# Six hand-overs to the FFN's down projection, a sixth weight buffer, and a first rstd by columns in a two-layer trunk

## The chip, the cores and the metric

The kernel runs on one core of a Trainium2 chip. The metric is the device time of one execution in microseconds; less is better. A core has a matrix engine (TensorE, PE in the profile; PEld is its weight load, which overlaps), a vector engine (VectorE, DVE), an engine for activation functions (ScalarE, ACT), a general engine (GpSimd, POOL) and a sync engine (SP) that here only issues loads and stores. Each engine takes its own instructions in the order of the program, and waits on semaphores for the results of the others. Matmuls write to PSUM, eight banks of 128 x 512 f32 values; everything else lives in SBUF.

## What is computed

The input is 512 tokens of 1024 channels. Two layers each have a mixer and a gated FFN with a short causal convolution, each behind an RMS norm and added to the residual; a final RMS norm closes. Cut to what matters here:

```python
def rms_norm(x, g):
    y = x * lax.rsqrt(jnp.mean(x * x, axis=-1, keepdims=True) + EPS)
    return y * g

def gated_conv_ffn(x, w_gate, w_up, conv_w, conv_b, w_down):   # w_gate, w_up: 1024 x 2816
    g = jnp.einsum('bsd,df->bsf', x, w_gate)
    g = causal_dwconv3(g, conv_w) + conv_b
    up = jnp.einsum('bsd,df->bsf', x, w_up)
    return jnp.einsum('bsf,fd->bsd', jax.nn.silu(g) * up, w_down)

for layer in range(2):
    xn = rms_norm(h, norm_mix[layer])
    h = h + (mixer_a_and_b(xn) if layer == 0 else mixer_c(xn))   # each with an output projection
    hn = rms_norm(h, norm_ffn[layer])
    h = h + gated_conv_ffn(hn, w_ffn_gate[layer], w_ffn_up[layer], conv_ffn[layer],
                           b_conv_ffn[layer], w_ffn_down[layer])
return rms_norm(h, final_norm)
```

Mixer A and B of layer 0 begin with one input projection; its last 512 columns, z, are normalized, pooled over windows of 2, 4, 8 and 16 tokens and multiplied by small matrices.

## The kernel before, in words

The residual stands transposed in SBUF: `h[k]`, eight tiles of 128 channels x 512 tokens. Every f32 operand of a matmul is split into a high and a low part (`hi`, `lo`: ScalarE rounds, VectorE subtracts, or a DMA adds), and a product is three matmuls: hi x hi, hi x lo, lo x hi (`mm3`, lines 134 to 137). A norm is not applied first: `Norm.add` splits h times the gain into `hg[k]`, and the factor rstd of a token is multiplied in after the projection. `Norm.square` sums the squares over the eight tiles into `ssq`, ScalarE squaring and GpSimd adding (L190, L191). With `apart=True` the last square stays in a tile of its own. From there, `rstd` makes all 512 factors in one row form, the same on all partitions, with two matmuls against a matrix of ones (L200, L201) and full-width VectorE passes (`inv_sqrt`, L242 to L251). `rstd_tokens` makes them as four columns, with small matmuls against a column of ones (L211, L212), and `rstd_spread` turns these into the row form by four transposes (L219) and a copy (L222). Layer 0's mixer uses `rstd`; both FFNs use the other two. `z_done` evacuates the z groups: it takes rstd at its first call, copies the bank (L406), multiplies (L407) and pools.

The FFN's 2816 hidden channels are 22 tiles, worked on in pairs f = 0, 2, ... 20. `Ffn.hidden(f)` makes one pair's activations:

- f = 0 (`direct`, not normed): 96 matmuls of gate and up weights with unnormalized `hg`, during which the columns of rstd are made and spread. Then `normalize` is issued for four pairs of channel tiles (it rewrites `hg` with the normalized input and prepares sums), and only then `rest()`, the evacuation: bank times rstd (L555), three taps of the convolution (L504, L506), silu (L512), times rstd on GpSimd (L558), times the up bank (L561), and the split into a_hi and a_lo (`act`, L261, L263).
- f = 2 (`direct`, normed): 96 matmuls, which need the normalized `hg`.
- f >= 4 (`seven`): the up product by seven half-size products (L663), the gate product as before.

`PARTS` says after which pairs the down projection runs: its entries (a, b) are ranges of tiles. In layer 0 `project` multiplies the part's activations with its down weights and adds into `h` (L306), in two halves of four output tiles. In layer 1 `group8` does the same with tokens as rows, eight outputs, and adds into `y` (L923). Both go through the first len - tail tiles with all outputs interleaved, then finish output by output; tail is 4.

What sets the order: the program's text is not the order of execution. A scheduler orders each engine's instructions ahead of time, and tile pools bound what it may do. A pool's tile with `bufs=n` is a ring, handed out in the order of the text: the next request waits until the use n requests before is over. So the matmul banks (`mm`, seven in the ring, and one more, `aux`) are handed out in the order of the text, and so are the split weights (`whi` and `wlo`, five each), the raw weights (four) and the activations (`ahi`, `alo`, six). On the engines nothing overtakes at run time. The queues: SP issues the loads of weights, GpSimd the DMAs that add for some low parts (L123, L595).

```python
PARTS = ((0, 6), (6, 12), (12, 18), (18, 22))
```

Of the kernel before, what the change touches and what calls it, by code (L numbers as in the profile page):

```python
# [8 lines left out]
F32 = mybir.dt.float32  # L9
F32R = mybir.dt.float32r  # L10
BF16 = mybir.dt.bfloat16
AF = mybir.ActivationFunctionType
ALU = mybir.AluOpType
PSUM = bass.MemoryType.PSUM

P = 128
D = 1024
S = 512
# [6 lines left out]
PAD = 16  # L25
# [5 lines left out]
def tile_trunk(ctx: ExitStack, tc: tile.TileContext, x, norm_mix, norm_ffn, final_norm,  # L31
# [16 lines left out]
    def aux_bank(name):  # L48
        return ps_aux.tile([P, 512], F32, tag="aux", name=name)
# [10 lines left out]
    small = cp.tile([P, LINE], F32, name="small")  # L60
    ones = small[:, :1]
    nc.gpsimd.memset(ones, 1.0)
    ones_r = cp.tile([P, P], F32R, name="ones_r")
    nc.gpsimd.tensor_copy(ones_r, ones.to_broadcast([P, P]))
    def params0():
        return params("0", [
            ("ca", conv_rows(conv_a[0]), 12), ("psc", rows_of(pool_scale[0]), 4),
# [17 lines left out]
    def params(layer, rows_, queue=nc.sync):  # L85
        rows = sum(n for _, _, n in rows_)
        pk = cp.tile([P, P], F32, tag="pk", bufs=1, name=f"pk{layer}")
        at, views = 0, {}
        for key, ap, n in rows_:
            queue.dma_start(pk[at : at + n, :], ap)  # L90
            views[key] = at
            at += n
        ps = aux_bank(f"prm_ps{layer}")
        nc.tensor.transpose(ps[:, :rows], pk[:rows, :], ident[:rows, :rows])
        sb = cp.tile([P, P], F32, tag=f"prm{layer}", name=f"prm{layer}")
        nc.vector.tensor_copy(sb[:, :rows], ps[:, :rows])

        def col(key, i):
            return sb[:, views[key] + i : views[key] + i + 1]

        return col
# [15 lines left out]

    def summed(raw, a, b, name):

        hi = wp.tile([P, a, b], F32R, tag="whi", bufs=5, name=f"whi_{name}")  # L120
        lo = wp.tile([P, a, b], F32R, tag="wlo", bufs=5, name=f"wlo_{name}")
        nc.scalar.activation(lo, raw, AF.Copy, scale=-1.0)  # L122
        nc.gpsimd.dma_start(lo, raw, accum_op=ALU.add)  # L123
        nc.scalar.activation(hi, raw, AF.Copy)
        return hi, lo

    def parts(raw, a, b, name):
        hi = wp.tile([P, a, b], F32R, tag="whi", bufs=5, name=f"whi_{name}")
        lo = wp.tile([P, a, b], F32R, tag="wlo", bufs=5, name=f"wlo_{name}")
        nc.scalar.activation(hi, raw, AF.Copy)  # L130
        nc.vector.tensor_tensor(lo, raw, hi.bitcast(F32), ALU.subtract)  # L131
        return hi, lo
# [6 lines left out]
    def group(name, outs, ks, lhs, rhs, tail, on_done, before=None, at_end=None):  # L139

        banks = {}
        head = len(ks) - tail
        order = [(i, j) for i in range(head) for j in outs]
        order += [(i, j) for j in outs for i in range(head, len(ks))]
        at = -1
        for i, j in order:
            if i > at and before is not None:
                before(ks[i])
            at = max(at, i)
            if j not in banks:  # L150
                banks[j] = mm_bank(f"{name}_{j}")
            mm3(banks[j], lhs(ks[i], j), rhs(ks[i], j), i == 0, i == len(ks) - 1)
            if i == len(ks) - 1 and at_end is None:
                on_done(j, banks[j])
        if at_end is not None:
            at_end()
            for j in outs:
                on_done(j, banks[j])
# [9 lines left out]
    class Norm:  # L168
# [13 lines left out]
        def square(self, k, order=lambda ins: ins):  # L182
            if self.n == 0:
                order(nc.scalar.activation(self.ssq, h[k], AF.Square))
            elif self.n == NK - 1 and self.apart:
                self.last = tp.tile([P, S], F32, tag="last", bufs=1, name=f"last_{self.name}")
                order(nc.scalar.activation(self.last, h[k], AF.Square))
            else:
                sq = tp.tile([P, S], F32, tag="sq", name=f"sq_{self.name}{k}")
                order(nc.scalar.activation(sq, h[k], AF.Square))  # L190
                nc.gpsimd.tensor_tensor(self.ssq, self.ssq, sq, ALU.add)  # L191
            self.n += 1

        def rstd(self):
            ps = aux_bank(f"ss_{self.name}")
            hi = tp.tile([P, S], F32R, tag="sq", name=f"ssh_{self.name}")
            lo = tp.tile([P, S], F32R, tag="sq", name=f"ssl_{self.name}")
            nc.scalar.activation(hi, self.ssq, AF.Copy)
            nc.vector.tensor_tensor(lo, self.ssq, hi.bitcast(F32), ALU.subtract)
            nc.tensor.matmul(ps, ones_r, hi, start=True, stop=False)  # L200
            nc.tensor.matmul(ps, ones_r, lo, start=False, stop=True)  # L201
            r = tp.tile([P, S], F32, tag="rstd", name=f"rstd_{self.name}")
            inv_sqrt(r, ps, S, self.name)
            return r

        def rstd_tokens(self):

# [139 lines left out]
    def mixer0():  # L347
        nonlocal prm0
        w = w_in_even[0]
        with tc.tile_pool(name="m0", bufs=1) as mp:  # L350
            prm_mix = params("mix", [("mix", rows_of(norm_mix[0]), NK)], nc.scalar)
            norm = Norm("m0", lambda k: prm_mix("mix", k))
            zchunks = {}
            xt = {}

# [12 lines left out]
            def turn(k):  # L368
                ps = mm_bank(f"xt_ps{k}")
                for t in range(NT):  # L370
                    nc.tensor.transpose(ps[:, t * P : (t + 1) * P], xt[k][:, t, :], ident)
                if k in raws:
                    raw, a, b, name = raws.pop(k)
                    hi = wp.tile([P, a, b], F32R, tag="whi", bufs=5, name=f"whi_{name}")
                    lo = wp.tile([P, a, b], F32R, tag="wlo", bufs=5, name=f"wlo_{name}")
                    for i in range(a):
                        zchunks[k + i] = hi[:, i, :], lo[:, i, :], raw[:, i, :]
                whi, wlo, wraw = zchunks[k]
                inorder(nc.scalar.activation(whi, wraw, AF.Copy))
                inorder(nc.vector.tensor_copy(h[k], ps))  # L380
                g = prm_mix("mix", k)
                inorder(nc.scalar.activation(hg[k][0], h[k], AF.Copy, scale=g))
                inorder(nc.vector.tensor_tensor(wlo, wraw, whi.bitcast(F32), ALU.subtract))
                inorder(nc.vector.scalar_tensor_tensor(
                    hg[k][1], h[k], g, hg[k][0].bitcast(F32), op0=ALU.mult, op1=ALU.subtract))
                norm.square(k, inorder)
                if k == 0:
                    load(6, 2)
# [8 lines left out]
            pooled = {}  # L397
            rstd = [None]

            def z_done(g, ps):  # L400
                if rstd[0] is None:
                    rstd[0] = norm.rstd()
                win = WINDOWS[g]
                z = mp.tile([P, S + LINE], F32, tag="z", bufs=2, name=f"z{g}")[:, :W]
                nc.gpsimd.memset(z[:, :PAD], 0.0)
                nc.scalar.copy(z[:, PAD:], ps)  # L406
                nc.vector.tensor_tensor(z[:, PAD:], z[:, PAD:], rstd[0], ALU.mult)  # L407
                s, step = z, 1
                while step < win:
                    s2 = mp.tile([P, S + LINE], F32, tag="zs", bufs=3, name=f"zs{g}_{step}")[:, :W]  # L410
                    lo_c = 2 * step - 1
                    nc.vector.tensor_tensor(s2[:, lo_c:], s[:, lo_c:], s[:, lo_c - step : W - step],
                                            ALU.add)
                    s, step = s2, 2 * step
                pl = mp.tile([P, S], F32, tag="pl", bufs=2, name=f"pl{g}")
                nc.vector.scalar_tensor_tensor(pl, s[:, PAD:], 1.0 / win, z[:, PAD:],
                                               op0=ALU.mult, op1=ALU.subtract)
                e = win - 1
                nc.vector.tensor_tensor(pl[:, :e], s[:, PAD : PAD + e], inv_pos[:, :e], ALU.mult)
                nc.vector.tensor_tensor(pl[:, :e], pl[:, :e], z[:, PAD : PAD + e], ALU.subtract)  # L420
                pooled[g] = split(mp, pl, f"pl{g}", tag="mix", bufs=8)
# [50 lines left out]
            return nxt  # L472


    PARTS = ((0, 6), (6, 12), (12, 18), (18, 22))
    HALF = S // 2
    NP = NK // 2
    PAIRS = [k for i in range(NP) for k in (i, i + NP)]
# [8 lines left out]
    class Ffn:  # L487
# [25 lines left out]
            return s  # L513

        def act(self, ft, s):
            self.acts[ft] = split(self.ap, s, f"a{self.layer}_{ft}", tag="a", bufs=6)

        def pair_weights(self, f, order, by_dma=""):

# [88 lines left out]
        def seven(self, f):  # L608
# [3 lines left out]
            stat = {}  # L612

            def pair(name):
                return [wp.tile([P, 2, 4, P], F32R, tag=f"w{x}", bufs=5, name=f"w{x}_{name}_{n}")
                        for x in ("hi", "lo")]

            def halves(hi, lo, src):
# [328 lines left out]

    def group8(name, ks, lhs, rhs, tail, on_done):
        banks = {}
        head = len(ks) - tail  # L950
        order = [(i, j) for i in range(head) for j in range(8)]
        order += [(i, j) for j in range(8) for i in range(head, len(ks))]
        for i, j in order:
# [40 lines left out]
```

## Time and profile before

| | us |
|---|---|
| median of 3 runs | 1012.66 (1012.38 to 1012.75) |
| the profiled execution | 1013.46 |
| its span, first to last instruction | 1011.5 |
| mean granted TensorE clock | 0.997 |

The profile is of one execution. A line of a group tells: line, engine, operation, output <- inputs, form, count | busy time, mean ns of one | the engine's idle time before, and what ended it. In order of time, a line tells start and duration, and in brackets the idle time before it and what ended it. One matmul of 128 x 512 lasts 0.39 us from start to end, but the next one starts 0.227 us after it: they are pipelined. Where the time goes on TensorE, largest groups:

| work | matmuls | busy us |
|---|---|---|
| gate products, `g`, L135 to L137 | 864 | 337 |
| down products, `d` and `dn`, L135 to L137 | 1056 | 411 |

The busy column counts each matmul's whole length, so overlapping ones of different groups count more than once.

| stretch, us | what runs |
|---|---|
| 0 to 147 | layer 0, mixer; 7.8 to 36 the z group, rstd ready at 44.7 |
| 147 to 491 | layer 0, FFN; first pair to 171.2, second to 193.0, pair f = 4 to 214, first down projection 214 to 246.8 |
| 491 to 645 | layer 1, mixer |
| 645 to 1004 | layer 1, FFN; second pair 673.0 to 694.9, first down projection 715.8 to 748.6 |
| 1004 to 1011.5 | final norm's end and the last store |

### The profile page before, as it was taken

To read this page: it belongs to the slowest core of one execution; us is meant where nothing else is said; L and a number is where in the kernel's file an instruction comes from. 1 tells how busy PE (TensorE), PEld (TensorE's weight loads), DVE (VectorE), ACT (ScalarE), POOL (GpSimd) and SP (SyncE) were. 2 spreads that over 40 slices of the span, in tenths; PEclk is the share of its full clock that TensorE was granted. 3 is DMA by queue.
4 is the path that set the end of the run, shared out by engine and by line. 5 is a ranking of instruction groups with operands and counts; after the bars stand their busy time and mean duration, and the time that the engine had idled before them with its cause. 6 is when DMAs were issued, how large, how long until landed. Compare 5 with 4: busy or idle time off the path is not lost.

```text
span 1011.5 us, 13009 instructions
## 1 busy us (share of the span) xinstructions
PE 998.6 (99%) x5169; PEld 853.3 (84%) x5169; DVE 612.6 (61%) x882; ACT 471.5 (47%) x685; POOL 90.0 (9%) x101
## 2 busy tenths in 40 slices
PE   9999999999999999999999999999999999999997
PEld 6788888888998899889878888888888988998885
DVE  5997458864557366636833645396745654763667
ACT  6423446642454266236645444575425623650553
POOL 3141021200000000000300001111000000000000
PEclk9999999999999999999999999999999999999998
DMA  7432235442444344434333123354424433442432
GB/s 239 151 104 84 84 99 143 113 146 71 125 117 143 87 119 132 126 84 125 131 120 104 63 90 98 96 121 117 146 63 126 135 116 89 141 127 82 122 87 83
DMA packets 79303, 114.98 MB, mean 114 GB/s; under 512 B 4004, under 2 KB 53388, under 8 KB 79244
## 3 DMA queue, kind: packets, MB, share of 16 engines
q1 hardware_dynamic: 73580, 98.96, 30.7%
q0 software_dynamic: 4320, 13.63, 7.3%
q10 hardware_dynamic: 1344, 1.58, 0.5%
q8 instruction: 40, 0.66, 0.3%
q14 instruction: 19, 0.16, 0.1%
HBM read 98.42 MB, written 2.10 MB: 99 GB/s over the span
## 4 chain that ended last, share of the span: by engine, by line
PE 95%; DVE 3%; ACT 1%; issue 1%; DMA 1%; POOL 0%; DVEq 0%; ACTq 0%; POOLq 0%
PE ua L663 10%; PE g L135 7%; PE g L136 6%; PE g L137 6%; PE ue L663 5%; PE d L136 4%; PE dn L137 4%; PE dn L135 4%; PE d L137 4%; PE d L135 4%; PE dn L136 4%; PE gu L135 3%; PE gu L137 3%; PE gu L136 3%; PE ub L663 3%; PE u L135 1%
## 5 line engine op out<-in xcount | busy, mean ns | idle before, releaser
L135 PE MATMUL g<-hgh,whi_g 128*128 128x512 f32 x288 | 112.5, 391 | 0.0
L136 PE MATMUL g<-hgl,whi_g 128*128 128x512 f32 x288 | 112.5, 391 | 0.0
L137 PE MATMUL g<-hgh,wlo_g 128*128 128x512 f32 x288 | 112.1, 389 | 0.0
L130 ACT ACTIVATE whi_g<-raw_g 128x1024 fp32r<-128x1024 f32 x40 | 42.1, 1053 | 93.6 <-PE dn L137 57.3
L136 PE MATMUL d<-a_lo,whi_d 128*128 128x512 f32 x176 | 68.6, 390 | 0.0
L135 PE MATMUL dn<-whi_dn,a_hi 128*128 128x512 f32 x176 | 68.6, 390 | 0.0
L136 PE MATMUL dn<-wlo_dn,a_hi 128*128 128x512 f32 x176 | 68.5, 389 | 0.0
L506 DVE SCALAR_TENSOR_TENSOR c<-rows,prm,c 128x512 f32<-128x512 f32 x88 | 68.1, 793 | 0.6
L137 PE MATMUL d<-a_hi,wlo_d 128*128 128x512 f32 x176 | 68.5, 389 | 0.0
L137 PE MATMUL dn<-whi_dn,a_lo 128*128 128x512 f32 x176 | 68.3, 389 | 0.0
L135 PE MATMUL d<-a_hi,whi_d 128*128 128x512 f32 x176 | 68.3, 390 | 0.0
L131 DVE TENSOR_TENSOR wlo_g<-raw_g,whi_g 128x1024 fp32r<-128x1024 f32 x40 | 48.8, 1221 | 28.3 <-ACT whi_g L130 28.3
L137 PEld LDWEIGHTS g<-hgh,wlo_g 128*128 128x128 f32 x288 | 54.1, 188 | 11.9 <-DVE wlo_g L131 0.5
L123 POOL DMA_DIRECT2D wlo_u<-raw_u x18 | 15.4, 857 | 536.3 <-ACT wlo_u L122 200.1
L135 PEld LDWEIGHTS g<-hgh,whi_g 128*128 128x128 f32 x288 | 54.2, 188 | 10.3
L136 PEld LDWEIGHTS g<-hgl,whi_g 128*128 128x128 f32 x288 | 54.2, 188 | 9.8
L620 DVE TENSOR_TENSOR wlo_a<-raw_u,whi_a 128x512 fp32r<-128x512 f32 x18 | 12.5, 692 | 82.6 <-ACT whi_a L619 82.6
L681 ACT COPY kept<-ua 128x256 f32<-128x256 f32 x54 | 19.8, 367 | 74.3 <-PE ua L663 74.3
L131 DVE TENSOR_TENSOR wlo_d<-raw_d,whi_d 128x1024 fp32r<-128x1024 f32 x22 | 26.9, 1221 | 35.1 <-ACT whi_d L130 35.1
L131 DVE TENSOR_TENSOR wlo_dn<-raw_dn,whi_dn 128x1024 fp32r<-128x1024 f32 x22 | 26.8, 1220 | 35.1 <-ACT whi_dn L130 35.1
L923 DVE TENSOR_TENSOR y<-dn,y 128x512 f32<-128x512 f32 x32 | 22.1, 689 | 42.9 <-PE dn L137 42.9
L619 ACT ACTIVATE whi_s<-s 128x1024 fp32r<-128x1024 f32 x36 | 38.1, 1057 | 19.9 <-PE d L136 14.2
(326 smaller groups left out, 2756.7 us busy)
## 6 DMA issues: line engine op xcount, KB each, us to landing
raw_u<-in_w_ffn_up_dram SPq DMA_DIRECT2D x36, 512.0 KB
raw_g<-in_w_ffn_gate_dram SPq DMA_DIRECT2D x36, 512.0 KB
raw_d<-in_w_ffn_down_dram SPq DMA_DIRECT2D x22, 512.0 KB
raw_dn<-in_w_ffn_down_dram SPq DMA_DIRECT2D x22, 512.0 KB
wlo_u<-raw_u POOLq DMA_DIRECT2D x18, 512.0 KB, 4.6
raw_oe<-in_w_out_even_dram SPq DMA_DIRECT2D x8, 512.0 KB
raw_g<-in_w_ffn_gate_dram SPq DMA_DIRECT2D x16, 256.0 KB
raw_u<-in_w_ffn_up_dram SPq DMA_DIRECT2D x16, 256.0 KB
```

Of the source, the lines that this page charges most:

```text
L123: nc.gpsimd.dma_start(lo, raw, accum_op=ALU.add)
L130: nc.scalar.activation(hi, raw, AF.Copy)
L131: nc.vector.tensor_tensor(lo, raw, hi.bitcast(F32), ALU.subtract)
L135: nc.tensor.matmul(ps, lhs[0], rhs[0], start=start, stop=False)
L136: nc.tensor.matmul(ps, lhs[0], rhs[1], start=False, stop=False)
L137: nc.tensor.matmul(ps, lhs[1], rhs[0], start=False, stop=stop)
L506: nc.vector.scalar_tensor_tensor(c, t[:, i : S + i], prm("cf", i * NF + ft), c, op0=ALU.mult, op1=ALU.add)
L619: nc.scalar.activation(hi, src, AF.Copy)
L620: nc.vector.tensor_tensor(lo, src, hi.bitcast(F32), ALU.subtract)
L663: nc.tensor.matmul(ps, l, r, start=at not in opened, stop=end, skip_group_check=True)
L681: nc.scalar.copy(kept[:, i, :], ps)
L923: nc.vector.tensor_tensor(dst, ps, dst, ALU.add)
```

## The change

`PARTS` has six entries. The first is the first pair alone, the others have four tiles. Since `len - tail` would be negative for the first, both loops take `max(0, ...)`. The activations' ring goes from six to four tiles, the rings of split weights from five to six. The matrix of ones and `rstd` are removed; layer 0's mixer takes `rstd_tokens` when the first z group is done and `rstd_spread` when the third is, and z's first two groups are only copied until then, and pooled after. The spare row of the last square and one of the parameter tiles share the space of others. Cut to its core:

```diff
-    ones_r = cp.tile([P, P], F32R, name="ones_r")
-    nc.gpsimd.tensor_copy(ones_r, ones.to_broadcast([P, P]))
...
-        sb = cp.tile([P, P], F32, tag=f"prm{layer}", name=f"prm{layer}")
+        sb = cp.tile([P, P], F32, tag="prm0" if layer == "0" else "prm1", name=f"prm{layer}")
...
     def parts(raw, a, b, name):
-        hi = wp.tile([P, a, b], F32R, tag="whi", bufs=5, name=f"whi_{name}")
-        lo = wp.tile([P, a, b], F32R, tag="wlo", bufs=5, name=f"wlo_{name}")
+        hi = wp.tile([P, a, b], F32R, tag="whi", bufs=6, name=f"whi_{name}")
+        lo = wp.tile([P, a, b], F32R, tag="wlo", bufs=6, name=f"wlo_{name}")
...
     def group(name, outs, ks, lhs, rhs, tail, on_done, before=None, at_end=None):
-        head = len(ks) - tail
+        head = max(0, len(ks) - tail)
...
             elif self.n == NK - 1 and self.apart:
-                self.last = tp.tile([P, S], F32, tag="last", bufs=1, name=f"last_{self.name}")
+                self.last = tp.tile([P, S], F32, tag="rstd", name=f"last_{self.name}")
...
-        def rstd(self):
-            ps = aux_bank(f"ss_{self.name}")
-            hi = tp.tile([P, S], F32R, tag="sq", name=f"ssh_{self.name}")
-            lo = tp.tile([P, S], F32R, tag="sq", name=f"ssl_{self.name}")
-            nc.scalar.activation(hi, self.ssq, AF.Copy)
-            nc.vector.tensor_tensor(lo, self.ssq, hi.bitcast(F32), ALU.subtract)
-            nc.tensor.matmul(ps, ones_r, hi, start=True, stop=False)
-            nc.tensor.matmul(ps, ones_r, lo, start=False, stop=True)
-            r = tp.tile([P, S], F32, tag="rstd", name=f"rstd_{self.name}")
-            inv_sqrt(r, ps, S, self.name)
-            return r
...
-            norm = Norm("m0", lambda k: prm_mix("mix", k))
+            norm = Norm("m0", lambda k: prm_mix("mix", k), apart=True)
...
+            zs = {}
+
+            def z_copy(g, ps):
+                zs[g] = mp.tile([P, S + LINE], F32, tag="z", bufs=2, name=f"z{g}")[:, :W]
+                nc.gpsimd.memset(zs[g][:, :PAD], 0.0)
+                nc.scalar.copy(zs[g][:, PAD:], ps)
+
             def z_done(g, ps):
-                if rstd[0] is None:
-                    rstd[0] = norm.rstd()
-                win = WINDOWS[g]
-                z = mp.tile([P, S + LINE], F32, tag="z", bufs=2, name=f"z{g}")[:, :W]
-                nc.gpsimd.memset(z[:, :PAD], 0.0)
-                nc.scalar.copy(z[:, PAD:], ps)
+                if g == 0:
+                    norm.rstd_tokens()
+                elif g == 2:
+                    rstd[0] = norm.rstd_spread()
+                    z_pool(0)
+                    z_pool(1)
+                z_copy(g, ps)
+                if g > 1:
+                    z_pool(g)
+
+            def z_pool(g):
+                win, z = WINDOWS[g], zs[g]
                 nc.vector.tensor_tensor(z[:, PAD:], z[:, PAD:], rstd[0], ALU.mult)
...
-    PARTS = ((0, 6), (6, 12), (12, 18), (18, 22))
+    PARTS = ((0, 2), (2, 6), (6, 10), (10, 14), (14, 18), (18, 22))
...
         def act(self, ft, s):
-            self.acts[ft] = split(self.ap, s, f"a{self.layer}_{ft}", tag="a", bufs=6)
+            self.acts[ft] = split(self.ap, s, f"a{self.layer}_{ft}", tag="a", bufs=4)
...
             def pair(name):
-                return [wp.tile([P, 2, 4, P], F32R, tag=f"w{x}", bufs=5, name=f"w{x}_{name}_{n}")
+                return [wp.tile([P, 2, 4, P], F32R, tag=f"w{x}", bufs=6, name=f"w{x}_{name}_{n}")
                         for x in ("hi", "lo")]
...
     def group8(name, ks, lhs, rhs, tail, on_done):
-        head = len(ks) - tail
+        head = max(0, len(ks) - tail)
```

The scheduler places the first part's down projection, in both layers, directly behind the first pair's 96 matmuls on TensorE and ahead of the second pair's.

More of the change, by code (lines that the diff above doesn't have):

```diff
@@ L127, in parts @@
     def parts(raw, a, b, name):
-        hi = wp.tile([P, a, b], F32R, tag="whi", bufs=5, name=f"whi_{name}")
-        lo = wp.tile([P, a, b], F32R, tag="wlo", bufs=5, name=f"wlo_{name}")
+        hi = wp.tile([P, a, b], F32R, tag="whi", bufs=6, name=f"whi_{name}")
+        lo = wp.tile([P, a, b], F32R, tag="wlo", bufs=6, name=f"wlo_{name}")
         nc.scalar.activation(hi, raw, AF.Copy)
@@ L373, in turn @@
                     raw, a, b, name = raws.pop(k)
-                    hi = wp.tile([P, a, b], F32R, tag="whi", bufs=5, name=f"whi_{name}")
-                    lo = wp.tile([P, a, b], F32R, tag="wlo", bufs=5, name=f"wlo_{name}")
+                    hi = wp.tile([P, a, b], F32R, tag="whi", bufs=6, name=f"whi_{name}")
+                    lo = wp.tile([P, a, b], F32R, tag="wlo", bufs=6, name=f"wlo_{name}")
                     for i in range(a):
```

## The prediction

> **What bounds the kernel now.** I read the page first, then TensorE's waits, then stretches of the two FFN stages, then single instructions in order of time where the change cuts in. First the page (busy us, share, instructions) and TensorE's waits (us in total, times, longest):
>
> ```profile
> span 1011.5 us, 13009 instructions
> ...
> PE 998.6 (99%) x5169; PEld 853.3 (84%) x5169; DVE 612.6 (61%) x882; ACT 471.5 (47%) x685; POOL 90.0 (9%) x101
> ```
>
> ```profile
> PE wst L764 <- POOL ws L757: 1.5, 1, 1.5
> ...
> PE z L135 <- ACT hgh L382: 1.0, 2, 0.8
> PE z L136 <- DVE hgl L384: 0.8, 1, 0.8
> ```
>
> TensorE is the bound: its last matmul starts at 1003.6, and it lacks work for about 5 us before that. No wait in either FFN is even listed. So nothing inside the FFNs can be gained by a faster hand-over or earlier weights, and any wait that the change puts on TensorE is paid in full, since no later idle time can pay it back. The stretches around the first two FFN pairs (us, then busy us of each engine; the clock is the column after POOL):
>
> ```profile
> 171.00:193.00 22.00, 22.00 (x99) 18.22 (x98) 22.00 (x34) 17.57 (x27) 6.98 (x6) 1.00 0.49 112
> 673.00:695.00 22.00, 22.00 (x99) 18.23 (x98) 22.00 (x34) 17.80 (x27) 6.96 (x6) 1.00 0.50 119
> 1004.00:1011.00 7.00, 0.00 (x0) 0.00 (x0) 3.24 (x10) 1.01 (x4) 0.00 (x0) 0.66 0.27 100
> ```
>
> In 171 to 193 TensorE runs the 96 matmuls of the second pair (f = 2), 21.8 us, or 0.227 us each. VectorE is just as full: it finishes the normalization and makes the first pair's activations. The second layer's 673 to 695 is the same to 0.02 us. In the last row the clock falls once TensorE is idle. Now the first pair's activations, start and duration in us:
>
> ```profile
> 170.99 0.39 PE L137 MATMUL gu<-hgh,wlo_u 128*128 128x512 f32 x1
> 171.21 0.39 PE L135 MATMUL gu<-hgh,whi_g 128*128 128x512 f32 x1
> ```
>
> ```profile
> 175.34 0.69 DVE L555 TENSOR_TENSOR rows<-gu,rstd_f 128x512 f32<-128x512 f32 x1
> ...
> 178.47 0.75 DVE L506 SCALAR_TENSOR_TENSOR c<-rows,prm,c 128x512 f32<-128x512 f32 x1
> ...
> 179.84 1.28 ACT L512 ACT_TABLE_LOAD   x1
> ...
> 181.13 0.72 ACT L512 ACTIVATE s<-c,prm 128x512 f32<-128x512 f32 x1
> ...
> 181.94 1.98 POOL L558 TENSOR_TENSOR s<-s,rstd_f 128x512 f32<-128x512 f32 x1 [1.50 <-ACT s L512]
> ```
>
> ```profile
> 185.10 0.63 ACT L261 ACTIVATE a_hi<-s 128x512 fp32r<-128x512 f32 x1 [1.05 <-DVE s L561]
> 185.76 0.73 ACT L512 ACTIVATE s<-c,prm 128x512 f32<-128x512 f32 x1
> 186.31 0.68 DVE L263 TENSOR_TENSOR a_lo<-s,a_hi 128x512 fp32r<-128x512 f32 x1
> ...
> 186.56 1.58 POOL L558 TENSOR_TENSOR s<-s,rstd_f 128x512 f32<-128x512 f32 x1 [2.65 <-ACT s L512]
> ...
> 189.35 0.62 ACT L261 ACTIVATE a_hi<-s 128x512 fp32r<-128x512 f32 x1
> ...
> 190.48 0.68 DVE L263 TENSOR_TENSOR a_lo<-s,a_hi 128x512 fp32r<-128x512 f32 x1
> ```
>
> At 171.21 the loads change from up weights to gate weights: the first pair's last matmul is out and the second pair begins. The first pair's two activations, each a high and a low part, are complete only at 191.2, 20 us later. Before the change nobody asks for them until 214, when the first down projection starts.
>
> **The change, part by part.** *The first part, (0, 2).* The down projection of part one needs only activations 0 and 1, and its 48 matmuls now stand on TensorE directly behind the first pair's 96 and ahead of the second pair's 96; so the built program orders them, in both layers. TensorE takes its instructions in order, so at 171.2 it waits for a chain that has just begun, and the 21.8 us of the second pair, its cover until now, is queued behind the wait.
>
> When is the chain done? VectorE has the same work ahead of L555 as before (the whole normalization of the pairs, with two weight splits), without a gap in the trace, so L555 stays at 175.3. The table load, silu, GpSimd product and first high part follow at the times shown: the other VectorE work put in between (two splits of down weights, 1.22 each, and L631, 0.69) is 3.1 us against 3.3 us now (L620, L131, L631, L633). So the first a_hi ends at 185.7. In the new order the taps of the second pair (L506, 1.78 at its longest) no longer stand between, so the second GpSimd product, ending 188.1, is taken up at once: product 0.68, high part 0.62, low part 0.68 bring the last low part to 190.1. Ten of the 48 matmuls fit in before that; the other 38 take 38 x 0.227 = 8.6 us, to 198.8. Unhindered, the 48 would be done at 171.2 + 10.9 = 182.1. So 16.7 us are lost.
>
> *The clock behind that wait.* TensorE does nothing for 14.5 us. At the end of the run the clock record falls to 0.5 within 2.3 us of the last matmul (hence 0.66 in the row above), and at the start the eight warming matmuls of 1.25 to 4.85 step by 0.43 us where they later would by half, full rate being recorded from 6.15, 4.9 us after the first. The fed matmuls resume at 185.8; full rate may come by 190.7. The few cold matmuls queued at 190 and the tail of the ramp cost 1.0 us as an estimate; bounds 0, and 2.5 if the ramp begins only at 190 and runs 4.9 us at half rate. [...]
>
> Bounds for one layer: below, the bare chain with no queue on VectorE or ScalarE (0.69 + 0.73 + 2 x 0.75 + 1.28 + 0.72 + 1.29 + 0.68 + 0.63 + 0.68 = 8.2 for the first activation, some 2.5 more for the second, done at 181.9), a loss of 8.5; above, today's 191.2 and the full ramp, 20.2. I take 17.7, near the upper end, as the queue on VectorE is the same one. Two layers: 35.4.
>
> *The other boundaries.* Parts of four have no leading columns: one output after another, all four activations. Parts (18, 22) have this form today, in both layers, behind the same preceding pair, and TensorE has no gap over 0.04 us there; so 0 for eight new places. The cover is that the first two activations (12 matmuls, 2.7 us) run while the last are split; without it about 1 us each. Two more parts in each layer add 32 additions into h and y (L306, L923) at 0.69 us, 22 us on VectorE, which is 61% busy and has a bank's 1.4 us or more for each; hidden. The queue of weight loads keeps its number of transfers and bytes.
>
> *The sixth weight buffer.* Splits can start one tile earlier. No TensorE wait on weights is in the FFNs to be removed: 0. Four activation buffers where six were: every part has at most four, and the next part's are made 20 us after its first matmuls: 0.
>
> *First rstd by columns.* Gone: two matmuls of 0.227, and six VectorE passes over 512 columns (0.68 + 0.69 + 3.35 + 3 x 0.69 = 6.8 us, with the 3.35 us reciprocal). Added: eight column matmuls, which at 149.86 to 151.56 in the FFN's norm take 1.7 us, and four transposes, 0.4. TensorE never waits for this rstd, so earlier columns earn nothing. The column matmuls stand between 31.0 and 33.7, where 0.8 us is idle for L384, and one ahead of the 0.8 us wait for L382: about 1.3 us is covered. Sum +0.4; bounds -1.6 (both waits go) and +1.7 (nothing covered).
>
> The total is 35.4 + 0.4 = 35.8 us on the span of 1011.5, so 1047.3. This execution took 1013.46, 2.0 outside the span; the runs' median of 1012.66 is 0.8 below it. On the median: 1048.5.
>
> **Rivals.** (1) The chain is shorter, because an emptier ScalarE and VectorE let the evacuation begin at 171: for it, TensorE's banks are ready then; against it, the normalization stands ahead on VectorE with no gap. At 8.5 a layer, 1012.7 + 17.4 = 1030. (2) The four-part boundaries wait too: about 1 us at eight places on top, 1056.5; for it, only 2.7 us of cover; against it, today's (18, 22). (3) Not slower: the second pair's matmuls in fact run ahead of the first down projection, or the hand-over has some equal cover. It decides from 19 us of cover on (171.2 to 190.1); 21.8 us would do, the loss would be 0, and the time 1013, or 1011 if both early waits vanish as well. For it, the text of the loops allows the hand-over late; against it, the order on TensorE.
>
> **How the numbers follow.** The forecast has 0.82, (1) 0.07, (2) 0.05, (3) 0.06. The likeliest's own range is 1042 (14.5 a layer) to 1054 (20.2 and +1.0). I widen it by a little to 1040 to 1055. A measurement tells about 0.2% from no change, 2 us: slower has 0.94, same 0.03 and faster 0.03, both from (3).
>
> **What would show it.** The profile should list two TensorE waits of some 14.5 us for the first a_hi (near 171 and 673) with shorter ones behind for the low part and the second activation, the clock below 1 in those stretches, busy time near 1000, no wait at 247 or later parts, and rstd_m some 6 us earlier than 44.7 without a gain. I am wrong if gate matmuls fill 171 to 193, if L555's successor starts well before 175, or if later stages end early by more than 1 us.

## The result, and the profile after

The changed kernel takes 1049.23 us (median of 4 runs, 1048.75 to 1049.7), the kernel before 1012.7 beside it. The ratio is 1.0361 (95% interval 1.0343 to 1.0379). The profiled execution took 1049.16 us with a span of 1047.1, which is 35.6 more than before.

The page of the changed kernel, then TensorE's waits (us in total, times, longest):

```profile
span 1047.1 us, 13089 instructions
...
PE 1006.0 (96%) x5187; PEld 856.9 (82%) x5187; DVE 626.6 (60%) x913; ACT 471.4 (45%) x685; POOL 85.0 (8%) x99
...
PEclk9999998899999999999999999979999999999999
```

```profile
PE d L133 <- ACT a_hi L247: 15.4, 3, 14.2
PE dn L133 <- ACT a_hi L247: 14.7, 2, 14.3
PE xt_ps L357 <- DMA xt<-in_x_dram: 1.4, 1, 1.4
PE clock L56 <- DVE idle L53: 1.3, 1, 1.3
PE z L134 <- DVE hgl L370: 0.9, 2, 0.8
```

The two new rows, 30.1 us together, are waits for the activations of the first hand-over in each layer, but for 0.75 us in a later part; the FFNs had no row at all before. The clock row, all nines before except for the last digit, shows 8 and 8 around the first hand-over and 7 at the second. TensorE's busy time has grown by 7.4 us although only 18 matmuls more are recorded: some of them are longer. Where, the stretches around the first hand-over show (length, busy us of PE, PEld, DVE, ACT, POOL, the granted clock, DMA share, GB/s):

```profile
171.60:186.00 14.40, 0.27 (x2) 0.00 (x0) 14.40 (x25) 10.72 (x17) 5.32 (x5) 0.62 0.61 121
186.00:192.00 6.00, 5.49 (x11) 3.48 (x12) 4.88 (x8) 1.36 (x3) 1.50 (x1) 0.50 0.17 59
192.00:200.60 8.60, 8.60 (x39) 7.04 (x38) 5.35 (x8) 0.68 (x2) 0.00 (x0) 0.99 0.17 61
200.60:222.40 21.80, 21.80 (x98) 18.06 (x97) 8.88 (x10) 7.91 (x11) 0.00 (x0) 1.00 0.15 49
691.20:705.40 14.20, 0.00 (x0) 0.00 (x0) 14.20 (x25) 10.49 (x17) 5.29 (x5) 0.59 0.63 121
```

TensorE idles for 14.4 us while VectorE is full (14.40 of 14.40). Then 6 us at half clock follow, with 11 recorded matmuls. From 200.6 the second pair's 21.8 us run, which had covered this chain before. The same is seen from TensorE's own instructions (start, duration; in brackets the idle time before and what ended it):

```profile
186.06 1.22 PE L133 MATMUL d<-a_hi,whi_d 128*128 128x512 f32 x2 [14.20 <-ACT a_hi L247]
187.26 0.79 PE L134 MATMUL d<-a_lo,whi_d 128*128 128x512 f32 x1
187.85 0.63 PE L135 MATMUL d<-a_hi,wlo_d 128*128 128x512 f32 x1
188.28 0.63 PE L134 MATMUL d<-a_lo,whi_d 128*128 128x512 f32 x1
188.71 0.63 PE L135 MATMUL d<-a_hi,wlo_d 128*128 128x512 f32 x1
189.13 0.63 PE L133 MATMUL d<-a_hi,whi_d 128*128 128x512 f32 x1
190.21 1.22 PE L133 MATMUL d<-a_hi,whi_d 128*128 128x512 f32 x2 [0.44 <-ACT a_hi L247]
191.23 1.04 PE L134 MATMUL d<-a_lo,whi_d 128*128 128x512 f32 x2
...
192.34 0.39 PE L134 MATMUL d<-a_lo,whi_d 128*128 128x512 f32 x1
```

Cutting both spans at the same events gives the account. In layer 0 the first pair ends at 171.60 and the second begins at 200.53; less the 10.9 us of the 48 matmuls in between, 18.0 are lost. Layer 1's mixer is taken from its first matmul to the first of its FFN. In the kernel before that is from 501.95, where layer 0's last down projection ends on TensorE, and not from 491.

| stretch | us more than before |
|---|---|
| up to the first FFN matmul (147.14, now 147.53) | +0.4 |
| layer 0, first hand-over | +18.0 |
| layer 0, rest of the FFN | +1.3 |
| layer 1, mixer (143.81, now 142.05) | -1.8 |
| layer 1, first hand-over (691.02 to 719.67, less 10.9) | +17.8 |
| rest | -0.1 |
| sum | +35.6 |

### The profile page after: what moved, and what is told of

Read it like the earlier page. It is cut to its first block, busy times and chain, and to the rows that moved or that the text cites. A ratio compares the mean times of both kernels' runs of the same rounds, so it can differ in the third digit from the quotient of the medians.

```text
span 1047.1 us, 13089 instructions
## 1 busy us (share of the span) xinstructions
PE 1006.0 (96%) x5187; PEld 856.9 (82%) x5187; DVE 626.6 (60%) x913; ACT 471.4 (45%) x685; POOL 85.0 (8%) x99
## 4 chain that ended last, share of the span: by engine, by line
PE 92%; DVE 3%; DMA 3%; ACT 1%; issue 0%; SPq 0%; POOL 0%; DVEq 0%; ACTq 0%; POOLq 0%
PE ua L662 10%; PE g L133 6%; PE g L134 6%; PE g L135 6%; PE ue L662 5%; PE dn L133 4%; PE dn L134 4%; PE d L133 4%; PE dn L135 4%; PE d L134 4%; PE d L135 4%; PE gu L133 3%; PE gu L135 3%; PE gu L134 3%; PE ub L662 2%; PE v L133 1%
## 5 line engine op out<-in xcount | busy, mean ns | idle before, releaser
L505 DVE SCALAR_TENSOR_TENSOR c<-rows,prm,c 128x512 f32<-128x512 f32 x88 | 65.9, 771 | 0.6
L135 PEld LDWEIGHTS g<-hgh,wlo_g 128*128 128x128 f32 x288 | 54.1, 188 | 11.5
L619 DVE TENSOR_TENSOR wlo_s<-s,whi_s 128x1024 fp32r<-128x1024 f32 x36 | 44.0, 1223 | 23.6 <-ACT whi_s L618 23.6
L129 DVE TENSOR_TENSOR wlo_dn<-raw_dn,whi_dn 128x1024 fp32r<-128x1024 f32 x22 | 26.8, 1225 | 44.7 <-ACT whi_dn L128 44.7
L922 DVE TENSOR_TENSOR y<-dn,y 128x512 f32<-128x512 f32 x48 | 32.8, 690 | 33.7 <-PE dn L135 33.4
```

Source lines behind the costliest of these rows:

```text
L135: nc.tensor.matmul(ps, lhs[1], rhs[0], start=False, stop=stop)
L505: nc.vector.scalar_tensor_tensor(c, t[:, i : S + i], prm("cf", i * NF + ft), c, op0=ALU.mult, op1=ALU.add)
L619: nc.vector.tensor_tensor(lo, src, hi.bitcast(F32), ALU.subtract)
L922: nc.vector.tensor_tensor(dst, ps, dst, ALU.add)
```

## The experiments

**1. The hand-over late.** Everything of the change stays, but the first part's down projection is handed over after the second pair. For layer 0 (layer 1 alike):

```diff
                 for f in range(a, b, 2):
-                    ffn.hidden(f)
+                    if f > 2:
+                        ffn.hidden(f)
+                if a == 0:
+                    ffn.hidden(0)
+                    ffn.hidden(2)
```

> The changed kernel, with the first part's down projection handed over after the second pair (f = 2) in both layers; parts, buffers and rstd stay. Theory (the loss is TensorE waiting for the first pair's activations, because its cover of 21.8 us is queued behind): both waits of 14.2 and 14.3 us vanish, as 21.8 us exceed the 19 us chain; the time falls by 2 x 17.8 us to 1013.6, between 1011 and 1015. Rival (six hand-overs cost by themselves, a third of the loss for each added one or so): stays above 1035. Rival (sixth buffer or column rstd costs): stays at 1049.

Measured: 1013.25 us (1012.44 to 1014.8), ratio 1.0008 [0.9999, 1.0017], span 1010.6. The stretches of this kernel with the second pair and then the 48 matmuls:

```profile
171.50:193.30 21.80, 21.80 (x98) 18.05 (x97) 20.62 (x33) 16.49 (x26) 7.26 (x6) 1.00 0.52 121
193.30:204.20 10.90, 10.90 (x50) 9.03 (x49) 10.90 (x17) 4.93 (x7) 0.00 (x0) 1.00 0.26 86
```

TensorE has no gap, and the clock stays at 1.00. The whole loss is gone, with six parts, 32 more additions, the sixth buffer and the column rstd all in place. So the loss belongs to the place of these 48 matmuls and to nothing else in the change.

**2. Six parts alone.** The kernel before with the six parts, `max(0, ...)` and four activation buffers.

```diff
-    PARTS = ((0, 6), (6, 12), (12, 18), (18, 22))
+    PARTS = ((0, 2), (2, 6), (6, 10), (10, 14), (14, 18), (18, 22))
```

> The kernel before with the six parts and four activation buffers alone; five weight buffers and the old full-width rstd stay. Theory: the whole loss is here, 1048 +- 2, with two TensorE waits of about 14 us for the first high part. Rival (buffer or rstd carry a share): clearly under 1045.

Measured: 1051.11 us, ratio 1.0378 [1.0359, 1.0397], span 1048.9, 1.1 above the expected range. That is the whole loss and, by the span, 1.8 us more. This kernel's TensorE waits:

```profile
PE d L135 <- ACT a_hi L261: 14.7, 2, 14.3
PE dn L135 <- ACT a_hi L261: 14.4, 1, 14.4
...
PE dn L135 <- ACT whi_dn L130: 1.2, 1, 1.2
PE d L135 <- ACT whi_d L130: 1.0, 1, 1.0
```

The last two rows, waits for a split down weight, are new, and the changed kernel has none. They led to experiment 8.

**3. The two-tile part in the middle.** The changed kernel with another cut: if any part of two tiles waited as the first does, the place would not matter.

```diff
-    PARTS = ((0, 2), (2, 6), (6, 10), (10, 14), (14, 18), (18, 22))
+    PARTS = ((0, 4), (4, 8), (8, 10), (10, 14), (14, 18), (18, 22))
```

> The changed kernel with the same six parts in another order of sizes: four, four, two, four, four, four. The two-tile part stands behind a pair of the seven-product kind instead of the unnormalized first pair. Theory: what costs is the long chain behind the first pair under the full VectorE queue, not a part's being small; a two-tile part here waits only for add, product and split, about 2.5 us a layer, and the first part of four waits about 2 us for the second pair's activations: 1013.6 + 9 = 1022, range 1014 to 1026. Rival (a part of two tiles has no cover wherever it stands, 17.8 us a layer): 1045 or more.

Measured: 1032.75 us (1030.93 and 1034.58), ratio 1.0197 [1.0177, 1.0217], span 1029.1: a miss, above the range. TensorE waits 1.8 us for the first part and 4.1 to 4.2 for the two-tile part, in each layer. The stretches (the first three are the two-tile part of layer 0, the last two the first part of layer 1):

```profile
302.80:306.70 3.90, 0.00 (x0) 0.00 (x0) 3.90 (x7) 1.54 (x3) 0.00 (x0) 0.92 0.41 131
306.70:313.00 6.30, 6.21 (x14) 4.50 (x15) 3.65 (x7) 0.04 (x1) 0.00 (x0) 0.51 0.27 81
313.00:321.00 8.00, 8.00 (x37) 6.58 (x37) 4.89 (x7) 1.26 (x2) 0.00 (x0) 1.00 0.01 2
706.00:708.00 2.00, 1.00 (x4) 0.86 (x5) 2.00 (x4) 1.23 (x2) 0.00 (x0) 1.00 0.45 108
708.00:712.00 4.00, 4.00 (x19) 3.13 (x18) 3.20 (x6) 0.00 (x0) 0.00 (x0) 1.00 0.68 208
```

After the longer wait the clock is at half until 312.9 in layer 0 and 821.5 in layer 1, 6.1 and 4.8 us after the matmuls resume. The 48 matmuls take 14.2 us in layer 0 and 13.6 in layer 1 where 11.0 would do. Waits (5.9 and 6.0) and slow matmuls (3.2 and 2.6) make 17.7; the span grew by 17.6. The place matters, then: 12 us of wait in both layers here against 30 at the start. My expectation lacked the waits' second price, the clock.

**4. The column rstd alone**, in the kernel before.

```diff
-            norm = Norm("m0", lambda k: prm_mix("mix", k))
+            norm = Norm("m0", lambda k: prm_mix("mix", k), apart=True)
...
+                if g == 0:
+                    norm.rstd_tokens()
+                elif g == 2:
+                    rstd[0] = norm.rstd_spread()
+                    z_pool(0)
+                    z_pool(1)
```

> The kernel before with the column rstd in the first mixer alone (and the shared tiles); four parts, six activation buffers, five weight buffers. Theory: +0.4 us from TensorE's small matmuls, the VectorE passes that are saved are hidden: 1012 to 1014, no difference that can be measured. Rival (the earlier rstd is a gain of the 6 us by which it comes earlier): 1007. Rival (it carries part of the loss): above 1020.

Measured: 1012.8 us (1012.35 to 1014.7), ratio 1.0002 [0.9993, 1.0011], span 1011.3. No change that can be told.

**5. The activations before the normalization.** The changed kernel, but VectorE and ScalarE make the first pair's activations ahead of the normalization of the remaining tiles, not behind it. This shortens the chain of rival (1).

```diff
+                rest()
                 for kp in range(NP):
                     self.normalize(kp)
-                rest()
```

> The changed kernel with the first pair's evacuation issued ahead of the normalization instead of behind it; the first part stays behind the first pair. Theory (some 4 us of the chain are VectorE's normalization queue ahead of the first bank's product, and more of it lies between the chain's steps): product at once after the last matmul, last low part 5 to 7 us earlier, second pair not held up by the later normalization: 1035 to 1040. Rival (bare chain as in the forecast's lower bound, loss 8.5 a layer): 1031. Rival (the normalization that is put off holds up the second pair by as much): 1047 or more.

Measured: 1041.82 us, ratio 1.0293 [1.0264, 1.0323], span 1039.4; just above the range. This kernel's TensorE waits:

```profile
PE dn L133 <- ACT a_hi L247: 8.1, 1, 8.1
PE d L133 <- ACT a_hi L247: 8.0, 1, 8.0
PE dn L134 <- DVE wlo_dn L129: 3.5, 1, 3.5
...
PE d L134 <- DVE a_lo L249: 0.9, 1, 0.9
```

The first pair ends at 172.93 and the last low part at 183.92, 11.0 us later instead of 19.3. So 8 us of the chain were the queue on VectorE, as rival (1) supposed. But only 7.4 us of the time came back, not two times 8. A split of down weights now stands behind the normalization and makes TensorE wait 3.5 us in layer 1. The clock is at half for 13.7 us in layer 0, 7.7 of them after TensorE has resumed (6.1 in the changed kernel). The 48 matmuls, with the waits among them, take 15.5 and 17.9 us, and the start is 1.3 us longer.

**6. TensorE kept busy in the wait.** The changed kernel with 54 more matmuls, into a bank that nobody reads, between the first pair and the first down projection. This is meant to take the clock out of the price and to leave the wait.

```diff
+    def fill(name):
+        ps = mm_bank(f"fill_{name}")
+        for i in range(FILL):
+            nc.tensor.matmul(ps, hg[0][0][:, :P], hg[0][0], start=i == 0, stop=i == FILL - 1)
...
                     ffn.hidden(f)
+                if a == 0:
+                    fill("0")
```

> The changed kernel with 54 matmuls of 0.227 us into a bank that nobody reads (12.3 us), between the first pair and the first part's down projection, in both layers; the 14 us wait is so cut to about 2. More of the 48 matmuls are then ordered ahead of the second activation's (some 7, 1.6 us a layer). Theory (half clock behind the wait costs 1.0 us a layer): clock record stays at 1, 1049.2 - 2 x (1.0 + 1.6) = 1044. [...] Rival (full ramp of 4.9 us at half rate, 2.5 a layer): 1041.

Measured: 1043.63 us, ratio 1.0311 [1.0281, 1.0341], span 1041.9. The stretches (the filling matmuls, the remaining wait, the 48):

```profile
172.00:184.40 12.40, 12.40 (x56) 10.05 (x54) 12.40 (x22) 10.08 (x16) 5.17 (x5) 1.00 0.55 88
184.40:186.40 2.00, 0.07 (x1) 0.00 (x0) 2.00 (x4) 0.63 (x1) 0.18 (x1) 1.00 1.05 349
186.40:198.50 12.10, 11.36 (x49) 9.09 (x50) 9.95 (x15) 2.02 (x4) 1.52 (x1) 1.00 0.17 59
```

The clock stays at 1.00, and the loss falls from 18.0 to 15.6 us in layer 0 and from 17.8 to 15.7 in layer 1. Not all of this is the clock, because the added matmuls also changed the order in which the scheduler places the 48. TensorE at its two waits, and the stretch between them (the last row is of TensorE alone):

```profile
186.45 1.65 PE L134 MATMUL d<-a_hi,whi_d 128*128 128x512 f32 x6 [1.98 <-ACT a_hi L248]
...
190.61 1.20 PE L134 MATMUL d<-a_hi,whi_d 128*128 128x512 f32 x4 [0.69 <-ACT a_hi L248]
```

```profile
186.40:190.60 4.20, 3.47 (x14) 1.00 0.21 74
```

Here 14 of the 48 run ahead of the wait for the second activation. In the changed kernel it is 7, from 186.06 to 189.13 in the rows above, and in layer 1 the counts are the same. Seven more matmuls are worth 1.6 us, as I had expected. What is left for the halved clock is 0.8 us in layer 0 and 0.5 in layer 1.

**7. The same in the middle.** Experiment 3 with 14 such matmuls (`FILL = 14`, `if a == 8`) ahead of the two-tile part, to see whether the clock explains its miss.

> e3_two_tiles_mid with 14 such matmuls (3.2 us) in its wait of 4.1 us ahead of the two-tile part. Theory (the 48 matmuls of this part take 14.2 and 13.6 us instead of 10.9 to 11.0 because the clock is at half for 6.8 us after the wait): record stays at 1, the part takes 11.0, and 6 us are gained: 1026.5. Rival (they are slowed by their own waits for banks or weights): the part still takes 14, 1032.

Measured: 1026.51 us (1025.98 and 1027.05), ratio 1.0142 [1.0113, 1.0172], span 1025.2. The stretches of the two-tile part in layer 0, and of the first part in layer 1:

```profile
303.00:307.00 4.00, 3.14 (x15) 2.31 (x13) 4.00 (x7) 1.62 (x3) 0.00 (x0) 1.00 0.41 127
307.00:318.10 11.10, 11.08 (x49) 9.18 (x50) 8.37 (x13) 1.16 (x2) 0.00 (x0) 1.00 0.15 47
703.50:705.60 2.10, 1.44 (x6) 1.22 (x7) 2.10 (x3) 1.21 (x2) 0.00 (x0) 0.99 0.65 163
705.60:709.00 3.40, 3.40 (x9) 2.59 (x9) 2.07 (x4) 0.00 (x0) 0.00 (x0) 0.50 0.69 206
```

The two-tile part takes 11.2 us in both layers instead of 14.2 and 13.6. Here too the order of the 48 changed, but in experiment 3 TensorE has no wait among them that another order could fill. So extra matmuls that compute nothing make the kernel faster, and the slow matmuls of experiment 3 were the clock: 5.8 of the 8.7 us by which 17.7 exceeds the 9 that I had expected. The other 2.9 are waits longer than I had thought.

**8. Five split-weight buffers** in the changed kernel.

```diff
-        hi = wp.tile([P, a, b], F32R, tag="whi", bufs=6, name=f"whi_{name}")
-        lo = wp.tile([P, a, b], F32R, tag="wlo", bufs=6, name=f"wlo_{name}")
+        hi = wp.tile([P, a, b], F32R, tag="whi", bufs=5, name=f"whi_{name}")
+        lo = wp.tile([P, a, b], F32R, tag="wlo", bufs=5, name=f"wlo_{name}")
```

> The changed kernel with five buffers for split weights instead of six. Theory (in e2_parts_only two TensorE waits of 1.0 and 1.2 us for the second split of down weights, behind the second activation, come from the fifth buffer's reuse): those two waits are back, 1049.2 + 2 = 1051. Rival (the forecast's zero for the sixth buffer holds here too): 1049.

Measured: 1052.81 us (1051.65 to 1053.59), ratio 1.0401 [1.0383, 1.0418], span 1049.9, which is 2.8 longer than with six, and 1.8 us above what I had expected. The interval lies above that of the changed kernel (1.0343 to 1.0379). ScalarE's split and TensorE's matmul behind it:

```profile
195.60 1.06 ACT L128 ACTIVATE whi_d<-raw_d 128x1024 fp32r<-128x1024 f32 x1 [5.98 <-PE d L134]
```

```profile
196.71 0.51 PE L133 MATMUL d<-a_hi,whi_d 128*128 128x512 f32 x1 [0.96 <-ACT whi_d L128]
```

The split waits 6.0 us for a matmul of the same 48 to free its buffer, and TensorE then waits for the split: both stand still by turns. With six buffers all the weights of the part are split while TensorE waits for the activations.

**9. Five buffers with the late hand-over**, the edits of 1 and 8 together.

> e1_late with five buffers for split weights. Theory (the sixth buffer matters only where the down weights are wanted right behind the first pair; handed over behind the second pair they are not): same as e1_late, 1012.5 to 1014. Rival (it is worth 1 us at each first hand-over wherever that stands): 1015 or more.

Measured: 1013.6 us (1013.01 to 1014.61), ratio 1.0012 [1.0002, 1.0021], span 1012.2. By the intervals it can't be told from experiment 1. So the sixth buffer repairs part of the stall that the early hand-over makes, and has nothing to do without it. No kernel here is faster than the one before; 1 and 4 equal it.

## Why the prediction was right, point by point

*The first part: right in place, mechanism and sum, and nearly so in how the sum is split.* The forecast had 17.7 us a layer, and 18.0 and 17.8 were measured. Experiment 1 shows the mechanism: with the second pair as cover, nothing is left of it. The split, 16.7 for the wait and 1.0 for the clock, can be worked out from the changed kernel itself. In TensorE's order ten of the 48 matmuls stand ahead of the first that needs the last low part, as forecast. That part is ready at 190.87 (the last row of the views below). The other 38, at 0.227 us each, would then end at 199.5, and the second pair begins at 200.53. So the wait alone costs 17.0 (199.5 less 171.60 and 10.9) and the halved clock 1.0. In layer 1 nine stand ahead, the last low part is ready at 710.30, and the second pair begins at 719.67: 17.2 and 0.5. Experiment 6, less its change of order, gives 0.8 and 0.5 for the clock. The upper bound of 2.5 for a slow way back was not reached.

*The chain.* The first high part was forecast to end at 185.7 and ended at 186.0, as everything came 0.4 later. The last low part was forecast for 190.1 and ended at 190.9. ScalarE and VectorE in the changed kernel:

```profile
185.38 0.63 ACT L247 ACTIVATE a_hi<-s 128x512 fp32r<-128x512 f32 x1 [2.56 <-DVE s L560]
...
189.52 0.63 ACT L247 ACTIVATE a_hi<-s 128x512 fp32r<-128x512 f32 x1 [2.76 <-DVE s L560]
...
372.52 1.06 ACT L128 ACTIVATE whi_g<-raw_g 128x1024 fp32r<-128x1024 f32 x1 [1.95 <-DMA raw_g<-in_w_ffn_gate_dram]
373.49 0.61 ACT L247 ACTIVATE a_hi<-s 128x512 fp32r<-128x512 f32 x1
```

```profile
187.13 1.76 DVE L632 TENSOR_TENSOR s<-raw_u 128x512 f32<-128x512 f32 x1
188.81 0.68 DVE L560 TENSOR_TENSOR s<-gu,s 128x512 f32<-128x512 f32 x1
...
190.19 0.68 DVE L249 TENSOR_TENSOR a_lo<-s,a_hi 128x512 fp32r<-128x512 f32 x1
```

The step that failed is "taken up at once". A sum of raw up weights for the pair f = 4 (L632; the same step took 0.69 in the kernel before) stood where the tap had stood, ran beside GpSimd's second product (186.84 to 188.34) and took 1.76 us; the product was taken up 0.5 us after its end. The forecast had removed the slow instruction and not asked what takes its place. The 1.76 us are 1.07 more than the 0.69 before, which is also the median of the step's 18 executions in the changed kernel. In layer 1 it took 1.75 us at 706.56, again beside GpSimd's product (1.50 us from 706.27). But the 0.69 before, at 182.07, were beside a product of GpSimd too (1.98 us from 181.94). So what makes the step longer was not shown.

*The clock.* The forecast had full rate perhaps by 190.7. The record of the changed kernel has half clock until 192.1, six us after TensorE resumed and with TensorE not yet fully fed: 0.50 from 175.1 to 192.1, 17.1 us, and just as long in layer 1, from 693.9 to 710.95. Only 12 and 10 matmuls are recorded in these two stretches, and the price was the 1.0 and 0.5 above. The half-clock stretches read for the experiments are 3.4 us long (experiment 7, layer 1), 6.8 (experiment 3, layer 0) and 13.7 (experiment 5, layer 0). What ends such a stretch was not shown.

*The other boundaries: forecast 0, measured 1.3 us in all.* One of the eight new places waits, for 0.75 us at 374.67. The rows above show why: ScalarE waited 1.95 us for a gate weight's DMA (whi_g), with the high part a_hi queued behind it. The part took some 1.1 us longer than its like. Rival (2), a wait of 1 us at each of the eight, did not come.

*The sixth buffer: forecast 0, wrong for this kernel.* Experiment 8 puts it at 2.8 us of span, of which the two waits of 1.0 and 1.2 are seen; the rest was not traced, and the order of the 48 changed there too (6 instead of 7 ahead of the second wait in layer 0). The reason given, that no wait on weights was there to be removed, looked at the kernel before; the stall of the change itself makes one.

*The column rstd: forecast +0.4.* rstd_m is ready at 38.5 instead of 44.7, 6.2 us earlier, and nothing is gained by it, as forecast. The start is 0.4 us longer, but a wait for a load of x alone grew by 0.7 there; experiment 4 can't tell the whole from nothing.

*Not foreseen:* 1.8 us less in layer 1's mixer. The wait of 1.5 for `ws` is gone; GpSimd's select took 1.17 us instead of 1.99. This wait is 0.2 in experiments 1 and 4 and not listed in 2, so six parts alone and the column rstd alone both shorten it. What sets it was not isolated. The prediction named a later stage that ends early by more than 1 us as a sign against it, and here is one. That the total came within 0.7 us is in part luck: this -1.8 and the +1.3 of the other boundaries, neither foreseen, nearly cancel.

*The rivals.* (3), not slower, was decided by the cover, and 21.8 us of it do suffice (experiment 1). Of (1) the mechanism exists (experiment 5), but in the changed kernel the normalization stands ahead on VectorE, as the forecast held against it.

## What to carry to other kernels

Before work is handed over in smaller pieces, ask for each piece what stands between its last input and its first matmul on the in-order engine; a piece whose cover is queued behind it pays for its chain, here 18.0 and 17.8 us, where the same piece behind its cover paid nothing (experiment 1). Price a wait on TensorE twice, once for the time and once for the clock behind it. The second price was 2.6 to 3.2 us where all the matmuls behind the wait were ready (experiment 3), and 0.5 to 1.0 where they had to wait for a second activation anyway. An experiment that adds instructions can change the order of the others (14 of the 48 instead of 7 ahead of the second activation, experiment 6), so look at that order before its difference is put down to one cause. A buffer that gains nothing in one order (experiment 9) can be what limits the loss in another (by 2.8 us of span, experiment 8), so a part of a change is priced in the kernel that holds the rest of it.

## What was not expected of the hardware

A short wait can halve the clock, or not. In experiment 7 the wait of 1.82 us before the first part of layer 1 was followed by half clock (0.50) from 705.6 for 3.4 us, in which 9 matmuls are recorded; in experiment 3 the wait there was 1.81 us, the clock stayed at 1.00 in the rows from 706 on, and 19 matmuls are recorded in the 4 us from 708. A wait of 1.4 us for x near 6 us halved the clock until 11.5 in experiment 5 (0.51, and 10 matmuls recorded from 8 to 11.5) and did not in the changed kernel (1.00, and 19). In experiment 6 a wait of 1.98 us halved nothing: the clock is 1.00 in its rows above. So the length of the wait alone does not decide it. What does was not shown, as no run here moved a wait by a known amount. One of these kernels' spans may so hold or lack some 1.7 us, an estimate from the 3.4 us at 0.50 of experiment 7. Experiment 9's span is 1.6 above that of experiment 1, while the medians differ by 0.35; in its trace the clock is at half from 7.5 to 10.9 us (0.59 over 8 to 11.5), and in that of experiment 1 it is not (1.00).
